# Storing every second low weight part of the first token group for reuse, and new gather rates by stage, in a three-group gMLP, SSD and PEER block

## The chip, the cores and the metric

The kernel runs on one core of one Trainium2 chip. The metric is the device time of one execution in microseconds (us); smaller is better. TensorE (PE in the rows, PEld for its weight loads), VectorE (DVE), ScalarE (ACT), GpSimd (POOL) and SyncE (SP, which only issues transfers here) each run their own list of instructions in a fixed order and wait for each other by semaphores.

## The reference

One block over 1024 tokens with 1024 features, all in fp32:

```
h = x @ w_in                                   # uv, z, xbc, dt, gates
ya = gmlp_branch(uv, ...) @ gm_w_out           # gelu, layer norm, 128-token mixing
yb = ssd_branch(z, xbc, dt, ...) @ ssd_w_out   # conv, chunked scan, gated norm
x1 = layer_norm(ALPHA * x + (g0 * ya + g1 * yb) @ w_o)
q = x1 @ w_q                                   # 8 heads, two keys each
experts, gates = two-level top-16 of 128 x 128 keys, softmax
ch = sum over 128 chosen experts of gates * gelu(u_tab[e] . x1) * v_tab[e]
ple = sigmoid(x1 @ ple_w_gate + b) * (p @ ple_w_proj)
out = layer_norm(ALPHA * x1 + ch + ple)
```

## The kernel before

**Groups.** The tokens go through in three groups of 256, 384 and 384 (`GROUPS`). `front(gi)` does everything up to the choice of experts for one group. For the first two groups the experts are then gathered row by row from DRAM (`experts_u`, `experts_v`); for the third they are computed densely over all 16384 experts (`dense_scores`, `dense_gates`, `dense`). In the rows below, front 0 runs from 0 to 520 us, front 1 from 520 to 1345, front 2 from 1345 to 2600, the dense part up to 3673, and what is left to the end. Within a front I call the parts after what they compute: the gMLP part (`phase` 0), the SSD part (`phase` 1), the merge of both branches (also `phase` 1 before), the query part with `w_o`, `w_q` and `ple` (`phase` 2). Fronts 1 and 2 have these from 520, 712, 1066, 1140 and from 1345, 1548, 1922, 2005 us on. The gate tables of the third group (`phase` 3) start at about 2310, the dense part is `phase` 4.

**Weights.** Products are split for fp32 precision: every operand is a high part in float32r and a low part that holds the rest, and `mm3` multiplies three times (lines 155 to 157). `weights` loads one tile of 512 KB (`raw`, on SP's queue), ACT rounds it to `whi` (line 149), DVE subtracts to get `wlo` (line 150). There are 676 such tiles; the 140 tiles of a front come again in each of the three fronts, 12 of the 420 are half size. The tiles of the dense part (`peer_uT`, `peer_vd`) come once.

**Gathers.** One gather brings 128 rows of 4 KB (512 KB) by an indirect DMA that POOL issues (line 837) into one of 12 `row` tiles (`ring`). A gather of `peer_u` is used by one DVE product (line 856). Four gathers of `peer_v` are used by eight matmuls into `pacc` (line 898; the trace counts each of them as two, so a set of four gathers is a row `x16`). There are 640 of each, 256 of each for the first group and 384 for the second.

**The order.** `front` and `dense` are generators that yield the estimated cost of what they have just written. The loop at the end of `block_kernel` multiplies it by `SIDE[phase]` and writes as many gathers, at 1.47 us each, beside it:

```
for cost in front(gi):
    owed += cost * SIDE[phase[0]]
    ...
    while side and owed > 0:
        step = next(side[0], None)
```

What is still left when `dense` is done is written after it, and ends with `finish` of the last block (lines 800 to 809). A scheduler turns this into the engines' lists, by priority; `tc.high_priority(offset=n)` moves an instruction n places ahead. POOL's list holds gathers and a few plain loads, and a waiting one holds up those behind it.

Of the kernel before, what the change touches and what calls it, by code (L numbers as in the profile page):

```python
# [8 lines left out]
F32 = mybir.dt.float32  # L9
F32R = mybir.dt.float32r  # L10
# [10 lines left out]
KD = D // 128  # L21
# [19 lines left out]
CST = 300  # L41
AHEAD_W = (20, 20)
AHEAD_G = 40
LEAD = 50
UNIT = 5.35
SIDE = (0.82, 0.78, 0.80, 0.66, 0.78)
ALPHA = 2 ** 0.25
# [29 lines left out]
def rows(ap, off, n, parts=128, stride=0):  # L77
    return bass.AP(tensor=ap.tensor, offset=ap.offset + off, ap=[[stride, parts], [1, n]])
# [3 lines left out]
def block_kernel(ctx, tc, a, out):  # L82
# [54 lines left out]
    def split(hi, lo, src):  # L137
        A.copy(hi, src)  # L138
        V.tensor_sub(lo, src, hi.bitcast(F32))  # L139

    def weights(src, k, n):

        raw = wp.tile([128, k, n], F32, name="raw", tag="raw", bufs=4)
        hi = wp.tile([128, k, n], F32R, name="whi", tag="whi", bufs=3)
        lo = wp.tile([128, k, n], F32R, name="wlo", tag="wlo", bufs=3)
        with tc.high_priority(offset=AHEAD_W[0]):
            DMA.dma_start(raw, src)
        with tc.high_priority(offset=AHEAD_W[1]):
            A.copy(hi, raw)  # L149
            V.tensor_sub(lo, raw, hi.bitcast(F32))  # L150
        return hi, lo
# [36 lines left out]
    def normalize(x, st, pool):  # L188
# [13 lines left out]
    def prepare(gi):  # L202

        T = GROUPS[gi][0] * 128
        t0 = 128 * sum(g[0] for g in GROUPS[:gi])
        where = ("left", "right")[gi % 2]
        es = ExitStack()
        xp = es.enter_context(tc.tile_pool(name="xp", bufs=1, side=where))
        xh = xp.tile([128, KD, T], F32R, name="xh")
        xl = xp.tile([128, KD, T], F32R, name="xl")  # L210
        with tc.tile_pool(name="xr", bufs=4, side=where) as xr:
            for k in range(KD):
                raw = xr.tile([128, T], F32, name="xraw")
                DMA.dma_start(raw, a["xT"][:, k, t0:t0 + T])
                split(xh[:, k], xl[:, k], raw)
        tokens[gi] = es, xp, xh, xl

    def front(gi):
# [24 lines left out]
        with tc.tile_pool(name="ga", bufs=1, side=side_) as ga, \  # L243
# [14 lines left out]
            def steps():  # L258
                raw = wp.tile([128, KD, NCOL], F32, name="raw", tag="raw", bufs=4)
                DMA.dma_start(raw, a["w_dt"])  # L260
                dh = wp.tile([128, KD, NCOL], F32R, name="whi", tag="whi", bufs=3)
                dl = wp.tile([128, KD, NCOL], F32R, name="wlo", tag="wlo", bufs=3)
                split(dh, dl, raw)
# [9 lines left out]
                V.tensor_add(dt, pd, dtb[:, None, :].to_broadcast(sh))  # L273
                e, r, q = [ga.tile(sh, F32, name=n) for n in ("e", "r", "q")]
                A.activation(e, dt, AF.Abs)
# [102 lines left out]
        with tc.tile_pool(name="sa", bufs=1, side=side_) as sa, tc.tile_pool(name="sb", bufs=2, side=side_) as sb:  # L378
# [117 lines left out]
            def first_half():  # L496
                for j in range(8):
                    p = channel_major(a["ssd_w_out"][j, 0], yfh, yfl)
                    o = sb.tile([128, T], F32, name="yo")
# [60 lines left out]
        for c in range(NB):  # L560
            DMA.dma_start(x1[:, c], a["x"][t0 + c * 128:t0 + c * 128 + 128, :])
        plb = q0.tile([128, 1024], F32, name="plb")
        qa_es = ExitStack()
        lq = qa_es.enter_context(tc.tile_pool(name="lq", bufs=1, side=side_))
        lg = lq.tile([128, 1024], F32, name="lg")
        lb = lq.tile([128, 1024], F32, name="lb")
# [3 lines left out]
        DMA.dma_start(lb, rows(a["ln1_b"], 0, 1024))  # L570
        DMA.dma_start(plb, rows(a["ple_b_gate"], 0, 1024))
        ph = lq.tile([128, 2, T], F32R, name="ph")
# [12 lines left out]
        with tc.tile_pool(name="qa", bufs=1, side=side_) as qa, tc.tile_pool(name="qb", bufs=2, side=side_) as qb:  # L585
# [98 lines left out]
    def select(gi, c):  # L684
# [303 lines left out]
    def dense(gi, t0, NB, xh, xl):  # L988
        T = NB * 128
        with tc.tile_pool(name="ea", bufs=1) as ea, tc.tile_pool(name="eb", bufs=2) as eb, \  # L990
# [13 lines left out]
            def piece(i2):  # L1004
# [153 lines left out]
```

## Time and profile before

| | |
|---|---|
| median of 3 runs | 3757.99 us (3755.95 to 3758.19) |
| the profiled execution | 3754.28 us, its span 3752.6 us |
| PE busy | 3439.9 us, 92% of the span |
| DVE busy | 2935.7 us, 78% |
| moved by DMA | 1183.88 MB, 315 GB/s in the mean |

A row of the windows gives, for a stretch in us from the span's start, its length, the busy time of each engine with its instructions, the granted TensorE clock as a share of full speed, the mean busy share of the 16 DMA engines, and GB/s. A row of the timeline gives start, duration, engine, line, operation, tiles, and in brackets the engine's idle time before it and what ended it.

### The profile page before, as it was taken

To read this page: it belongs to the slowest core of one execution; us is meant where nothing else is said; L and a number is where in the kernel's file an instruction comes from. 1 tells how busy PE (TensorE), PEld (TensorE's weight loads), DVE (VectorE), ACT (ScalarE), POOL (GpSimd) and SP (SyncE) were. 2 spreads that over 40 slices of the span, in tenths; PEclk is the share of its full clock that TensorE was granted. 3 is DMA by queue.
4 is the path that set the end of the run, shared out by engine and by line. 5 is a ranking of instruction groups with operands and counts; after the bars stand their busy time and mean duration, and the time that the engine had idled before them with its cause. 6 is when DMAs were issued, how large, how long until landed. Compare 5 with 4: busy or idle time off the path is not lost. (4 is left out here: it accounts for less than half of the span.)

```text
span 3752.6 us, 59429 instructions
## 1 busy us (share of the span) xinstructions
PE 3439.9 (92%) x21390; PEld 2939.4 (78%) x21390; DVE 2935.7 (78%) x6823; ACT 1754.2 (47%) x2671; POOL 1569.2 (42%) x1310
## 2 busy tenths in 40 slices
PE   9899996999998988999987989889989999999995
PEld 8888896888887977888777878777768878778771
DVE  6677898898987989894698999997676676676652
ACT  6888443475752333475742334675333323233220
POOL 0000004744455444543455455334455455455544
PEclk9999998999999999999999999999999999999997
DMA  6444647989899787989899899899999999999987
GB/s 212 160 164 160 229 174 249 389 308 356 311 369 391 288 305 285 358 308 323 295 326 337 302 337 371 329 335 370 349 378 379 363 360 370 357 365 395 367 313 283
DMA packets 405703, 1183.88 MB, mean 315 GB/s; under 512 B 40736, under 2 KB 135968, under 8 KB 402336
## 3 DMA queue, kind: packets, MB, share of 16 engines
q0 software_dynamic: 187488, 682.71, 48.5%
q1 hardware_dynamic: 217200, 494.76, 36.8%
q8 instruction: 168, 2.75, 0.3%
q10 hardware_dynamic: 720, 2.62, 0.2%
q14 instruction: 127, 1.04, 0.1%
HBM read 1121.01 MB, written 58.92 MB: 314 GB/s over the span
## 5 line engine op out<-in xcount | busy, mean ns | idle before, releaser
L149 ACT CAST whi<-raw 128x1024 fp32r<-128x1024 f32 (+1 forms) x676 | 700.5, 1041 | 1127.2 <-PE mm L156 582.2
L837 POOL DMA_INDIRECT row<-in_peer_u_dram,idx x640 | 796.3, 1244 | 1004.3 <-PE pacc L898 376.2
L157 PE MATMUL mm<-xh,wlo 128*128 128x384 f32 (+2 forms) x3160 | 1055.3, 335 | 57.4 <-DVE wlo L150 50.5
L150 DVE TENSOR_TENSOR wlo<-raw,whi 128x1024 fp32r<-128x1024 f32 (+1 forms) x676 | 817.1, 1211 | 371.0 <-ACT whi L149 298.7
L155 PE MATMUL mm<-xh,whi 128*128 128x384 f32 (+2 forms) x3160 | 1060.6, 336 | 38.0 <-ACT whi L149 27.2
L156 PE MATMUL mm<-xl,whi 128*128 128x384 f32 (+2 forms) x3160 | 1046.8, 331 | 0.6 <-DVE xl L139 0.6
L837 POOL DMA_INDIRECT row<-in_peer_v_dram,idxT x640 | 758.9, 1186 | 681.9 <-DVE row L856 210.9
L856 DVE SCALAR_TENSOR_TENSOR row<-row,x1b 128x1024 f32<-128x1024 f32 x640 | 773.6, 1217 | 22.9 <-DMA row<-in_peer_u_dram,idx 18.5
L155 PEld LDWEIGHTS mm<-xh,whi 128*128 128x128 f32 (+1 forms) x3160 | 606.9, 192 | 93.4 <-ACT whi L149 51.5
L157 PEld LDWEIGHTS mm<-xh,wlo 128*128 128x128 f32 (+1 forms) x3160 | 606.1, 192 | 78.1 <-DVE wlo L150 60.1
L156 PEld LDWEIGHTS mm<-xl,whi 128*128 128x128 f32 (+1 forms) x3160 | 606.3, 192 | 9.5 <-issue 2.8
L898 PE MATMUL pacc<-row,zw 128*32 128x512 f32 x2560 | 321.3, 621 | 39.2 <-DMA row<-in_peer_v_dram,idxT 39.1
L155 PE MATMUL po<-whi,ewh 128*128 128x512 f32 x768 | 313.9, 409 | 20.1 <-DVE eacc L1051 17.9
L156 PE MATMUL po<-wlo,ewh 128*128 128x512 f32 x768 | 309.4, 403 | 17.1 <-DVE wlo L150 17.0
L157 PE MATMUL po<-whi,ewl 128*128 128x512 f32 x768 | 308.2, 401 | 0.0
L898 PEld LDWEIGHTS pacc<-row,zw 128*32 128x32 f32 x2560 | 68.5, 111 | 193.9 <-issue 140.6
L155 PEld LDWEIGHTS po<-whi,ewh 128*128 128x128 f32 x768 | 147.3, 192 | 86.3 <-DVE eacc L1051 19.9
L156 PEld LDWEIGHTS po<-wlo,ewh 128*128 128x128 f32 x768 | 147.5, 192 | 50.4 <-DVE wlo L150 18.5
L852 POOL DMA_DIRECT2D x1b<-x x5 | 3.0, 606 | 434.2 <-DMA x<-x 434.1
L138 ACT CAST ewh<-ew 128x384 fp32r<-128x384 f32 x128 | 65.6, 513 | 242.4 <-DVE ew L1019 175.3
L157 PEld LDWEIGHTS po<-whi,ewl 128*128 128x128 f32 x768 | 147.4, 192 | 36.1
L981 PE MATMUL mt<-o,o 128*128 128x128 f32 x768 | 148.9, 302 | 15.1 <-DVE o L979 6.0
(275 smaller groups left out, 5609.3 us busy)
## 6 DMA issues: line engine op xcount, KB each, us to landing
raw<-in_peer_uT_dram SPq DMA_DIRECT2D x128, 512.0 KB
raw<-in_peer_vd_dram SPq DMA_DIRECT2D x128, 512.0 KB
raw<-in_w_xbc_dram SPq DMA_DIRECT2D x96, 512.0 KB
raw<-in_w_g_dram SPq DMA_DIRECT2D x48, 512.0 KB
raw<-in_w_z_dram SPq DMA_DIRECT2D x48, 512.0 KB
raw<-in_ssd_w_out_dram SPq DMA_DIRECT2D x48, 512.0 KB
raw<-in_w_q_dram SPq DMA_DIRECT2D x48, 512.0 KB
g<-gt SPq DMA_DIRECT2D x24, 1024.0 KB
```

The costliest lines, as they stand in the source:

```text
L138: A.copy(hi, src)
L149: A.copy(hi, raw)
L150: V.tensor_sub(lo, raw, hi.bitcast(F32))
L155: PE.matmul(p, lhsT=lh, rhs=rh, start=start, stop=False, skip_group_check=skip)
L156: PE.matmul(p, lhsT=lh, rhs=rl, start=False, stop=False, skip_group_check=skip)
L157: PE.matmul(p, lhsT=ll, rhs=rh, start=False, stop=stop, skip_group_check=skip)
L837: g = POOL.indirect_dma_start(out=t, out_offset=None, in_=a[tab], in_offset=bass.IndirectOffsetOnAxis(ap=ix, axis=0))
L852: POOL.dma_start(x1, x1_d[gi, c])
L856: u = V.scalar_tensor_tensor(t, t, 1.0, x1, op0=OP.mult, op1=OP.mult, accum_out=act[:, k:k + 1])
L898: return PE.matmul(pacc[q * 32:q * 32 + 32, h * 512:h * 512 + 512], lhsT=zws[z][:, q, r % 4, :], rhs=ts[q][:, h * 512:h * 512 + 512], star ...
L981: PE.matmul(p[:, i, :], lhsT=o1, rhs=o2, start=True, stop=True)
```

## The change

In front 0 every second weight tile (`turn[0] % 2 == 0`) also stores its `wlo` to a DRAM tile of its own, by a DMA on POOL's queue. In fronts 1 and 2 a tile that is found in `kept` loads this `wlo` back, again on POOL's queue and 80 places ahead (`AHEAD_L`), instead of subtracting on DVE. `raw` and `whi` are as before. The one set of three `wlo` buffers becomes two sets of two: `wlo0` and `wlo1`. In front 0 and for the dense part's tiles the sets alternate; in fronts 1 and 2 loaded tiles use `wlo1` and subtracted ones `wlo0`. The gather rates `SIDE` change for four of the five stages, and the merge gets one of its own (`phase` 5). To make room, other tiles become fewer or are shared: `xraw` 4 to 3, `ewh` and `ewl` 13 to 11, `e`, `r`, `q`, `yo`, `plb` and `ixf` move into tiles that exist already.

```diff
-AHEAD_W = (20, 20)
+AHEAD_W, AHEAD_L = (20, 20), 80
-SIDE = (0.82, 0.78, 0.80, 0.66, 0.78)
+SIDE = (0.70, 0.82, 0.68, 0.66, 0.86, 1.1)
...
+        key = (src.tensor.name, src.offset)
+        keep = front_of[0] == 0 and turn[0] % 2 == 0
+        again = key in kept
         raw = wp.tile([128, k, n], F32, name="raw", tag="raw", bufs=4)
         hi = wp.tile([128, k, n], F32R, name="whi", tag="whi", bufs=3)
-        lo = wp.tile([128, k, n], F32R, name="wlo", tag="wlo", bufs=3)
+        turn[0] += 1
+        own = front_of[0] == 0 or "peer_" in src.tensor.name
+        at = turn[0] % 2 if own else int(again)
+        lo = wp.tile([128, k, n], F32R, name="wlo", tag=f"wlo{at}", bufs=2)
         with tc.high_priority(offset=AHEAD_W[0]):
             DMA.dma_start(raw, src)
+        with tc.high_priority(offset=AHEAD_L):
+            if again:
+                POOL.dma_start(lo, kept[key])
         with tc.high_priority(offset=AHEAD_W[1]):
             A.copy(hi, raw)
-            V.tensor_sub(lo, raw, hi.bitcast(F32))
+            if not again:
+                V.tensor_sub(lo, raw, hi.bitcast(F32))
+        if keep:
+            kept[key] = dram.tile([128, k, n], F32R, name=f"lo{turn[0]}")
+            POOL.dma_start(kept[key], lo)
...
+        phase[0] = 5
         mp_es = ExitStack()
...
-                ready[i2] = [eb.tile([128, T], F32R, name=n, bufs=I2B + 5) for n in ("ewh", "ewl")]
+                ready[i2] = [eb.tile([128, T], F32R, name=n, bufs=I2B + 3) for n in ("ewh", "ewl")]
```

POOL's list at the start of the gathers, in front 1, before (`x1b` is the block's input row, `idx` and `idxT` the expert numbers):

```order
L852 DMA x1b<-x_0_0_5316 128x1024
L852 DMA x1b<-x_0_1_5318 128x1024
L837 DMA row<-in_peer_u_dram,idx_0_7225 128x1024 x70
L837 DMA row<-in_peer_v_dram,idxT_0_7226 128x1024
L837 DMA row<-in_peer_u_dram,idx_0_7225 128x1024
```

and with the change (`lo_...` are the DRAM tiles):

```order
L160 DMA wlo<-lo_214 128x1024
L160 DMA wlo<-lo_280 128x1024
L160 DMA wlo<-lo_379 128x1024
L160 DMA wlo<-lo_467 128x1024
L160 DMA wlo<-lo_570 128x1024
L160 DMA wlo<-lo_652 128x1024
L861 DMA row<-in_peer_u_dram,idx_0_7360 128x1024 x5
L160 DMA wlo<-lo_736 128x1024
L861 DMA row<-in_peer_u_dram,idx_0_7360 128x1024 x5
L160 DMA wlo<-lo_820 128x1024
L861 DMA row<-in_peer_u_dram,idx_0_7360 128x1024 x5
L160 DMA wlo<-lo_912 128x1024
```

A load now stands after about every five gathers, 140 in all, and 70 stores stand ahead of the first gather.

DVE's list in the merge of front 1, before (`row` products are the gathers' users, `ya` and `ml` the merge itself):

```order
L150 TENSOR_TENSOR wlo<-raw,whi 128x1024
L139 TENSOR_TENSOR ml<-ya,mh 128x384
L150 TENSOR_TENSOR wlo<-raw,whi 128x1024
L856 SCALAR_TENSOR_TENSOR row,act<-row,x1b 128x1024
L545 TENSOR_TENSOR sg<-sg,rrow 128x384
L856 SCALAR_TENSOR_TENSOR row,act<-row,x1b 128x1024
L150 TENSOR_TENSOR wlo<-raw,whi 128x1024
L547 TENSOR_TENSOR ya<-ya,mm 128x384
L150 TENSOR_TENSOR wlo<-raw,whi 128x1024
```

and with the change:

```order
L164 TENSOR_TENSOR wlo<-raw,whi 128x1024
L880 SCALAR_TENSOR_TENSOR row,act<-row,x1b 128x1024
L569 TENSOR_TENSOR ya<-ya,mm 128x384
L911 COPY zw_139<-wT 64x4x4 x2
L570 TENSOR_TENSOR ya<-ya,sg 128x384
L571 TENSOR_TENSOR ya<-ya,m0t 128x384
L880 SCALAR_TENSOR_TENSOR row,act<-row,x1b 128x1024
L139 TENSOR_TENSOR ml<-ya,mh 128x384
L164 TENSOR_TENSOR wlo<-raw,whi 128x1024
```

Half of the subtractions are gone from between the others; over the whole program DVE has 676 of them before and 536 after.

The end of PE's list before (`po` are the last products of the dense part):

```order
L155 MATMUL po<-whi,ewh 128x512
L156 MATMUL po<-wlo,ewh 128x512
L157 MATMUL po<-whi,ewl 128x512
L898 MATMUL pacc<-row,zw_139 32x512 x32
L898 MATMUL pacc<-row,zw_138 32x512 x32
L898 MATMUL pacc<-row,zw_139 32x512 x32
```

and with the change:

```order
L172 MATMUL po<-whi,ewh 128x512
L173 MATMUL po<-wlo,ewh 128x512
L174 MATMUL po<-whi,ewl 128x512
L172 MATMUL po<-whi,ewh 128x512
L173 MATMUL po<-wlo,ewh 128x512
L174 MATMUL po<-whi,ewl 128x512
L922 MATMUL pacc<-row,zw_139 32x512 x16
```

Of 96 `pacc` matmuls (48 gathers) behind the last `po`, 16 (8 gathers) are left. By the same list the dense part holds those of 272 gathers of `peer_v` instead of 228, and all before it 360 instead of 364. The group of eight ahead of the last sixteen stands 18 `po` matmuls before the end.

## Rows read from the trace of the kernel before

**Rows 1.** The page: span, busy time, share and instructions of two engines.

```profile
span 3752.6 us, 59429 instructions
PE 3439.9 (92%) x21390; PEld 2939.4 (78%) x21390; DVE 2935.7 (78%) x6823; ACT 1754.2 (47%) x2671; POOL 1569.2 (42%) x1310
```

**Rows 2.** Windows, by stage.

```profile
0.00:520.00 520.00, 477.82 (x3807) 458.36 (x3808) 384.87 (x929) 367.05 (x597) 2.21 (x9) 0.97 0.55 186
520.00:712.00 192.00, 161.14 (x966) 153.53 (x965) 182.06 (x476) 72.04 (x95) 89.90 (x64) 0.92 0.74 272
712.00:1066.00 354.00, 341.85 (x2254) 300.99 (x2253) 313.47 (x620) 243.05 (x390) 172.87 (x143) 0.99 0.89 330
1066.00:1140.00 74.00, 70.46 (x417) 64.42 (x418) 61.47 (x101) 26.31 (x34) 42.60 (x35) 0.98 1.00 382
1140.00:1345.00 205.00, 187.27 (x1314) 162.75 (x1314) 176.23 (x571) 65.17 (x99) 97.02 (x79) 0.96 0.89 333
1345.00:1548.00 203.00, 178.71 (x1082) 153.70 (x1082) 190.02 (x580) 77.53 (x103) 100.94 (x79) 0.94 0.84 308
...
2005.00:2310.00 305.00, 272.59 (x1751) 243.25 (x1750) 285.64 (x965) 106.37 (x144) 147.29 (x119) 0.96 0.89 328
...
2600.00:3673.00 1073.00, 1026.32 (x5243) 811.89 (x5245) 702.88 (x1084) 325.69 (x435) 541.09 (x457) 0.97 0.97 363
3673.00:3752.60 79.60, 34.76 (x193) 6.47 (x192) 15.25 (x29) 5.63 (x7) 38.83 (x40) 0.68 0.77 291
```

**Rows 3.** Waits of PE from 520 to 2310 us: total, times, longest.

```profile
PE mm L157 <- DVE wlo L150: 51.3, 24, 14.2
...
PE mm L156 <- DVE wlo L150: 17.0, 8, 5.4
```

**Rows 4.** Windows around the longest of these waits, and of high traffic.

```profile
622.00:640.00 18.00, 5.20 (x17) 5.20 (x18) 18.00 (x43) 1.32 (x3) 5.00 (x4) 0.53 0.49 155
...
680.00:712.00 32.00, 32.00 (x183) 32.00 (x182) 32.00 (x50) 8.83 (x11) 27.43 (x16) 1.00 1.03 412
```

**Rows 5.** Timeline of PE at the end.

```profile
3672.38 0.40 PE L156 MATMUL po<-wlo,ewh 128*128 128x512 f32 x1
3672.62 0.39 PE L157 MATMUL po<-whi,ewl 128*128 128x512 f32 x1
3672.94 3.64 PE L898 MATMUL pacc<-row,zw 128*32 128x512 f32 x32
...
3738.09 2.96 PE L898 MATMUL pacc<-row,zw 128*32 128x512 f32 x16 [2.44 <-DMA row<-in_peer_v_dram,idxT]
```

**Rows 6.** Timeline of DVE at the end: the first instruction of the last finish.

```profile
3741.10 1.22 DVE L802 TENSOR_TENSOR x1b<-x1b,pacc 128x1024 f32<-128x1024 f32 x1 [43.87 <-PE pacc L898]
```

**Rows 7.** Timeline of PE within the dense part: one set of four gathers.

```profile
3651.98 1.92 PE L898 MATMUL pacc<-row,zw 128*32 128x512 f32 x16
```

**Rows 8.** The chain that ended last: longest and shortest of its five gathers.

```profile
3688.32 9.59 DMA row<-in_peer_v_dram,idxT
...
3731.78 6.26 DMA row<-in_peer_v_dram,idxT
```

**Rows 9.** The page's groups: the subtraction.

```profile
L150 DVE TENSOR_TENSOR wlo<-raw,whi 128x1024 fp32r<-128x1024 f32 (+1 forms) x676 | 817.1, 1211 | 371.0 <-ACT whi L149 298.7
```

**Rows 10.** Timeline of PE in front 1: the pace of a front's products.

```profile
616.17 0.34 PE L155 MATMUL mm<-xh,whi 128*128 128x384 f32 x1
616.35 0.34 PE L156 MATMUL mm<-xl,whi 128*128 128x384 f32 x1
```

**Rows 11.** Timeline of POOL: a plain load of 512 KB, and a gather.

```profile
3707.14 0.59 POOL L796 DMA_DIRECT2D row<-in_ln_g_dram  x1
...
3709.89 0.97 POOL L837 DMA_INDIRECT row<-in_peer_v_dram,idxT  x1 [0.30 <-issue]
```

**Rows 12.** Waits of POOL from 520 to 2310 us.

```profile
POOL row L837 <- DVE row L856: 274.9, 120, 12.0
POOL row L837 <- PE pacc L898: 274.6, 60, 10.8
```

More of the change, by code (lines that the diff above doesn't have):

```diff
@@ L139, in split @@
         V.tensor_sub(lo, src, hi.bitcast(F32))
+    kept, turn = {}, [0]
     def weights(src, k, n):
+        key = (src.tensor.name, src.offset)
+        keep = front_of[0] == 0 and turn[0] % 2 == 0
+        again = key in kept
         raw = wp.tile([128, k, n], F32, name="raw", tag="raw", bufs=4)
         hi = wp.tile([128, k, n], F32R, name="whi", tag="whi", bufs=3)
-        lo = wp.tile([128, k, n], F32R, name="wlo", tag="wlo", bufs=3)
+        turn[0] += 1
+        own = front_of[0] == 0 or "peer_" in src.tensor.name
+        at = turn[0] % 2 if own else int(again)
+        lo = wp.tile([128, k, n], F32R, name="wlo", tag=f"wlo{at}", bufs=2)
         with tc.high_priority(offset=AHEAD_W[0]):
             DMA.dma_start(raw, src)
+        with tc.high_priority(offset=AHEAD_L):
+            if again:
+                POOL.dma_start(lo, kept[key])
         with tc.high_priority(offset=AHEAD_W[1]):
             A.copy(hi, raw)
-            V.tensor_sub(lo, raw, hi.bitcast(F32))
+            if not again:
[3 more added lines that the diff above has]
+            POOL.dma_start(kept[key], lo)
         return hi, lo
@@ L195, in normalize @@
         A.activation(x, x, AF.Identity, scale=rs, bias=nm)
+    front_of = [None]
     ps, ps_es, phase, tk_, selects = {}, [None], [0], [None], []
@@ L210, in prepare @@
         xl = xp.tile([128, KD, T], F32R, name="xl")
-        with tc.tile_pool(name="xr", bufs=4, side=where) as xr:
+        with tc.tile_pool(name="xr", bufs=3, side=where) as xr:
             for k in range(KD):
@@ L231, in front @@
         phase[0] = 0
+        front_of[0] = gi
         tk_es = ExitStack()
@@ L261, in steps @@
                 dh = wp.tile([128, KD, NCOL], F32R, name="whi", tag="whi", bufs=3)
-                dl = wp.tile([128, KD, NCOL], F32R, name="wlo", tag="wlo", bufs=3)
+                dl = wp.tile([128, KD, NCOL], F32R, name="wlo", tag="wlo0", bufs=2)
                 split(dh, dl, raw)
@@ L273, in steps @@
                 V.tensor_add(dt, pd, dtb[:, None, :].to_broadcast(sh))
-                e, r, q = [ga.tile(sh, F32, name=n) for n in ("e", "r", "q")]
+                erq = gb.tile([128, T], F32, name="erq", tag="t1", bufs=3)
+                e, r, q = [erq[:, n * NB * NCOL:(n + 1) * NB * NCOL].rearrange("p (c h) -> p c h", c=NB)
+                           for n in range(3)]
                 A.activation(e, dt, AF.Abs)
@@ L498, in first_half @@
                     p = channel_major(a["ssd_w_out"][j, 0], yfh, yfl)
-                    o = sb.tile([128, T], F32, name="yo")
+                    o = sb.tile([128, T + 3], F32, name="xin")[:, :T]
                     A.copy(o, p)
@@ L561, in front @@
             DMA.dma_start(x1[:, c], a["x"][t0 + c * 128:t0 + c * 128 + 128, :])
-        plb = q0.tile([128, 1024], F32, name="plb")
+        lg = q0.tile([128, 1024], F32, name="lg")
         qa_es = ExitStack()
         lq = qa_es.enter_context(tc.tile_pool(name="lq", bufs=1, side=side_))
-        lg = lq.tile([128, 1024], F32, name="lg")
         lb = lq.tile([128, 1024], F32, name="lb")
@@ L570, in front @@
         DMA.dma_start(lb, rows(a["ln1_b"], 0, 1024))
-        DMA.dma_start(plb, rows(a["ple_b_gate"], 0, 1024))
         ph = lq.tile([128, 2, T], F32R, name="ph")
@@ L612, in front @@
             for u in range(16):
+                if u == 4:
+                    plb = lg
+                    DMA.dma_start(plb, rows(a["ple_b_gate"], 0, 1024))
                 p = channel_major(a["w_q"][u], xh, xl)
@@ L762, in select @@
             ixT = idxT_t[gi, c].rearrange("p (n q r) -> p n q r", n=PARTS, q=4)
-            ixf = [tk.tile([128, PARTS, PP], F32, name=f"ixf{p}") for p in range(PARTS)]
+            ixf = [wide.rearrange("p h k n -> p (h k n)")[:, p * 128:p * 128 + 128].rearrange(
+                "p (n k) -> p n k", n=PARTS) for p in range(PARTS)]
             for p in range(PARTS):
```

## The prediction

> **What bounds the kernel now.** The page first: PE is busy in 3439.9 of 3752.6 us, DVE in 2935.7 [rows 1]. A share over the whole span hides stages with different limits, so the windows come next. In the SSD part of front 1 PE is busy in 341.9 of 354 us and nothing can be won there but the products themselves. In the gMLP parts (520 to 712 and 1345 to 1548) and the query part of front 2, DVE is busy in 182 of 192, 190 of 203 and 286 of 305 us, PE in less, and the granted clock is 0.92, 0.94 and 0.96 [rows 2]. There PE waits for DVE: from 520 to 2310 us it waits 51.3 + 17.0 = 68.3 us, in 32 waits, for a `wlo` [rows 3]. The longest, 14.2 us, shows what follows one: in the 18 us around it DVE is busy all the time, and the granted clock is 0.53, that is mostly at 1.2 instead of 2.4 GHz [rows 4]. From 2600 us on PE is again the busiest, beside transfers at 363 GB/s [rows 2]. The last 79.6 us are another case: the dense part's products are done at 3673, and PE does 48 gathers' products as they land, busy in 34.8 us at a clock of 0.68 [rows 2, 5]. So the end is a tail of gathers with nothing beside it, and then the last finish, from 3741.1 to 3752.6, 11.5 us [rows 6].
>
> **The change, part by part.** The sum is made against the profiled execution, 3754.3 us.
>
> *The tail.* With the new rates 8 gathers of `peer_v` are left behind the last `po` instead of 48. The last gathers can't be issued at will: of the 12 `row` tiles four hold layer-norm rows by then, so the last four gathers wait for the set that stands 18 `po` matmuls ahead of the end, 18 x 0.24 = 4.3 us [rows 5]. From there four issues of 0.97 + 0.30 us [rows 11] and a landing of 6.3 to 9.6 us [rows 8], taken as 8, make 13; less the 4.3, 9 us behind the last `po`, then 1.9 us of products [rows 7] and the finish of 11.5 us. That is 22 us instead of 79.6: **-58**. (18 if the gathers land as fast as the fastest, 30 if the finish has to wait for the dense part's own layer norm.)
>
> *What the tail did is done elsewhere.* The dense part gets 44 gathers more, the fronts 4 fewer. A set of four costs PE 1.92 us at full clock [rows 7]: 11 sets are 21 us, one set less is 2: **+19**. The tail's products were no cheaper, but at the end there was nothing beside them.
>
> *The subtractions.* 140 fewer at 1.21 us [rows 9] take 140 x 1.21 = 169 us (a little less, since 8 are half as long) from DVE, spread over fronts 1 and 2, where it is the busier engine in three stages. On the path they are worth at most what PE waits for them: 68.3 us [rows 3]. Every second tile no longer asks DVE at all, and for the others DVE has half the backlog; but its other work (gather products, top-16) stays, and with the same waits for ACT's `whi`. Ends 0 and 68; I take half, **-34**. The rates of the gMLP and query parts, lower now, work the same way and are in this half.
>
> *The clock.* In the four stages where it is 0.92 to 0.96 it costs 15 + 8 + 12 + 12 = 48 us (192 x 0.08, 205 x 0.04, 203 x 0.06, 305 x 0.04) [rows 2]. About half of PE's idle time there is these waits, so some 24 us hang on them; with half of the waits gone **-12** (0 to -24).
>
> *The loads.* No operation like them stands in the trace at this place; the nearest is a plain load on the same queue, 0.59 us of POOL with 0.3 of issue [rows 11], and 6.3 to 9.6 us from issue to landing for a gather of the same size [rows 8]. POOL is busy in 97 to 173 us of stages of 205 and 354 us [rows 2], so 140 x 0.9 = 126 us have room. What counts is whether a load lands in time. `wlo1` has two buffers, so a load waits until the loaded tile four places earlier is used up, and three tiles of 24 products lie ahead of its use: 72 x 0.176 = 12.7 us at the pace of [rows 10]. Less 0.9 and 8 that leaves 4 us. In token-major stretches some have only about two tiles ahead, 9 us, and are late by around 1 us; a late one costs its clock too. Nothing if all are in time; with some 15 late by under 1 us, **+12**. Behind a load that waits for its buffer the gathers wait as well. That is covered: POOL already waits 275 us for DVE's products and 275 us for `pacc` in these fronts, up to 12.0 us at a time [rows 12], so gathers run well ahead of use; without that cover each load would hold up a row's product by its wait.
>
> *Traffic.* 136 x 0.524 + 4 x 0.262 = 72 MB are loaded in fronts 1 and 2 and half of that is stored in front 0. Front 0 runs at 186 GB/s [rows 2]; 36 MB over 520 us add 70, beside an idle POOL. In the SSD part of front 1 some 33 loads (17 MB in 354 us) add 49 to 330 GB/s; in its merge, with the rate of 1.1, 382 GB/s would go beyond the 412 GB/s that a stretch with PE busy throughout shows [rows 2, 4], and what doesn't fit moves into the query part, where there are 333 and fewer gathers now. Slower landings and a store that holds a `wlo` in front 0: 0 to +40, taken **+7**. The smaller sets (`xraw`, `ewh`, `ewl`) and shared tiles (`yo`, `plb`, `ixf`, `erq`) I cost at nothing: ACT is busy in 326 of 1073 us of the dense part [rows 2] and hides a later cast. If it doesn't, each of the 16 steps loses up to the 4.3 us of 18 `po`, 70 us in all.
>
> Here a rule of the Trainium skill speaks against the change. The rows show 412 GB/s over 32 us with PE never idle, and 363 over the dense part [rows 2, 4]. "DMA: Bandwidth & Descriptors", section "Where 436 GB/s comes from", says that for transfers between HBM and SBUF the HBM share of a core, about 358 GB/s, binds. This case's trace doesn't agree for a core that streams alone; by that rule the end would be an estimated 3770 us (the fourth rival's sum with 358), so slower, and by the rows the queues still have room.
>
> Sum: -58 + 19 - 34 - 12 + 12 + 7 = -66, so 3688 against 3754.3. The median of the runs, 3758.0, is 3.7 above the profiled execution; I forecast **3692** for it.
>
> **The rivals.** A change of under 0.2% (7.5 us) is what a measurement of this kernel can't tell from none.
>
> 1. *The loads give back what the subtractions gave.* DVE is relieved, but PE waits for loads as long as it did for `wlo`, mostly in the gMLP parts, where gathers wait for a DVE that is 95% busy and loads stand behind them. Then only the tail is left: -58 + 19 + 3 = -36, **3722**. For it: the small margin of 4 us. Against it: three tiles of lead, and less work on DVE.
>
> 2. *The loads are late: slower than before.* One mechanism: POOL works its list in order, a gather in front of a load waits up to 12.0 us for a DVE product [rows 12], and this eats the margin. 30 loads late by 4 us, with half-clock stretches behind them, take 30 x 4 = 120 instead of 12: 3692 + 108 = **3800**. It decides from some 20 such loads on (66 + 12 = 78 us). Against it: most of POOL's waits are those of gathers that are ahead.
>
> 3. *More is won.* All 68 us and 24 of clock, and loads in time: -58 + 19 - 92 + 3 = -128, **3630**.
>
> 4. *The queues become the bound.* All bytes after 520 us are 1183.9 - 97 (186 GB/s x 520 us) = 1087 MB, and 72 more are 1159. At the dense part's 363 GB/s these take 3193 us: 520 + 3193 + 12 = **3725**. Against it: the 412 GB/s.
>
> 5. *The gain and a few late loads cancel:* half of the second rival's price, **3750 to 3765**.
>
> **How the numbers follow.** The forecast (3655 to 3715) 0.57; rival 1, 0.13; rival 4, 0.08; rival 3, 0.07; rival 5, 0.04; rival 2, 0.11. Faster by over 0.2%: 0.57 + 0.13 + 0.08 + 0.07 = 0.85; the same 0.04; slower 0.11. The range of 3640 to 3762 leaves out the second and most of the third rival, 0.17; the forecast's own is the 3655 to 3715.
>
> **What would show it.** In the trace of the changed kernel: from the last `po` to the end 18 to 30 us, no long row of `pacc` waits there; dense part some 20 us longer or less, by what its waits do; `wlo` of DVE as a cause of PE's waits from 520 to 2310 at some 34 us instead of 68; a new cause, DMA `wlo<-lo`, at some 10 us; granted clock of the gMLP parts 0.95 or more; DMA at 370 to 390 GB/s in fronts 1 and 2. The prediction is wrong if DMA `wlo<-lo` is PE's first cause of waits, if `pacc` waits for rows before the end, or if the dense part shows waits for `ewh`.

## The result and the profile after

The changed kernel takes 3733.41 us (median of 4 runs, 3723.69 to 3734.77), the kernel before beside it 3758.09 (4 runs, 3755.95 to 3761.96): a ratio of 0.9928, 95% interval 0.9913 to 0.9944. Faster, by 25 us where 66 were forecast. The profiled execution took 3733.71 us, its span is 3732.0.

The page of the changed kernel, lines that answer to [rows 1], and the line of its DMA packets:

```profile
span 3732.0 us, 59553 instructions
...
PE 3432.0 (92%) x21390; PEld 2941.5 (79%) x21390; DVE 2790.4 (75%) x6683; ACT 1752.4 (47%) x2672; POOL 1646.2 (44%) x1520
...
DMA packets 435944, 1292.43 MB, mean 346 GB/s; under 512 B 44096, under 2 KB 139328, under 8 KB 432576
```

DVE's 140 subtractions are gone (6823 to 6683 instructions) and it is busy 145 us less, and 108.5 MB are moved more: 36 stored and 72 loaded, as counted.

Windows of the changed kernel by stage: front 0 in four parts, front 1 from 551 to 1384, front 2 to 2344, both as one row, then dense part and tail.

```profile
0.00:125.00 125.00, 110.91 (x878) 108.31 (x879) 71.25 (x154) 67.95 (x95) 10.79 (x25) 0.97 0.80 267
125.00:371.00 246.00, 218.89 (x1711) 205.51 (x1709) 177.55 (x384) 215.44 (x376) 14.88 (x28) 0.94 0.64 208
...
423.00:551.00 128.00, 117.34 (x909) 112.78 (x909) 106.91 (x392) 59.40 (x96) 10.69 (x20) 0.96 0.82 280
551.00:723.00 172.00, 153.64 (x897) 146.27 (x897) 150.17 (x394) 69.54 (x92) 85.97 (x77) 0.95 0.88 329
723.00:1075.00 352.00, 336.08 (x2222) 294.81 (x2222) 287.48 (x597) 243.62 (x391) 190.91 (x172) 0.99 0.99 374
1075.00:1168.00 93.00, 78.78 (x469) 66.97 (x467) 56.93 (x102) 27.03 (x35) 52.43 (x51) 0.96 1.04 404
1168.00:1384.00 216.00, 197.82 (x1368) 176.05 (x1368) 165.31 (x592) 70.99 (x106) 97.51 (x95) 0.95 0.99 370
1384.00:1552.00 168.00, 158.06 (x966) 138.07 (x967) 158.28 (x510) 69.58 (x94) 93.08 (x82) 0.97 0.95 357
...
551.00:2344.00 1793.00, 1642.07 (x10561) 1452.82 (x10561) 1435.69 (x3790) 867.09 (x1302) 922.47 (x840) 0.97 0.97 362
...
2628.00:3711.00 1083.00, 1032.09 (x5310) 799.37 (x5312) 697.07 (x1076) 318.39 (x427) 564.77 (x495) 0.97 0.99 371
3711.00:3732.00 21.00, 4.23 (x33) 0.77 (x32) 14.28 (x25) 5.63 (x7) 0.52 (x1) 0.66 0.44 166
```

The same stretches of the kernel before, in rows that [rows 2] cut otherwise: front 0, fronts 1 and 2, the dense part.

```profile
0.00:531.00 531.00, 488.82 (x3901) 469.36 (x3902) 395.77 (x997) 370.55 (x602) 2.21 (x9) 0.97 0.55 187
...
531.00:2335.00 1804.00, 1652.34 (x10596) 1454.84 (x10594) 1576.60 (x3924) 867.02 (x1300) 882.33 (x710) 0.96 0.88 322
...
2628.00:3673.00 1045.00, 1002.72 (x5121) 791.35 (x5124) 690.77 (x1064) 318.53 (x426) 528.94 (x447) 0.98 0.97 362
```

In fronts 1 and 2 DVE is busy 141 us less, and the stretch is only 11 us shorter. PE stands idle there for 1804 - 1652 = 152 us before and 1793 - 1642 = 151 after; what is won are 10 us of PE's busy time, at a clock of 0.97 instead of 0.96. The column to read is the one ahead of GB/s: the queues' share went from 0.88 to 0.97.

Waits in the changed kernel: first PE, DVE and POOL from 551 to 2344, then, behind the last gap, PE in the dense part.

```profile
PE mm L174 <- DMA wlo<-lo: 15.5, 9, 3.9
PE mm L172 <- ACT whi L162: 14.8, 14, 3.3
PE mm L173 <- DMA wlo<-lo: 14.1, 3, 6.9
PE mt L805 <- DVE sel L753: 13.9, 4, 6.2
PE mt L467 <- DVE cbm L451: 13.3, 7, 3.9
PE mm L174 <- DVE wlo L164: 10.1, 10, 3.1
PE pacc L922 <- DMA row<-in_peer_v_dram,idxT: 10.1, 5, 3.8
...
PE mm L173 <- DVE wlo L164: 7.1, 3, 2.8
...
DVE row L880 <- DMA row<-in_peer_u_dram,idx: 40.1, 22, 3.7
...
POOL wlo L160 <- PE mm L174: 188.9, 65, 12.1
POOL row L861 <- PE pacc L922: 164.8, 60, 13.9
POOL row L861 <- DVE row L880: 157.8, 84, 7.2
...
PE po L172 <- DVE eacc L1075: 31.0, 7, 15.4
PE po L173 <- DVE wlo L164: 16.7, 5, 5.3
```

PE's 68.3 us of waits for a subtracted `wlo` [rows 3] are down to 17.2. What came instead: 29.6 us for a loaded `wlo`, and more waits for other work of DVE (`sel` 13.9 us, 2.7 before; `cbm` 13.3, 1.1 before). DVE itself waits 40.1 us for gathered rows; in the kernel before, from 530 to 2334, it was this:

```profile
DVE row L856 <- DMA row<-in_peer_u_dram,idx: 3.3, 3, 2.3
```

The end, on PE's timeline:

```profile
3710.61 0.40 PE L174 MATMUL po<-whi,ewl 128*128 128x512 f32 x1
3710.94 1.93 PE L922 MATMUL pacc<-row,zw 128*32 128x512 f32 x16
3716.36 2.37 PE L922 MATMUL pacc<-row,zw 128*32 128x512 f32 x16 [3.49 <-DMA row<-in_peer_v_dram,idxT]
```

The tail of [rows 5] is gone: 21 us from the last `po` to the end, with one wait of 3.49 us.

Stage lengths in us, of three pairs of profiled executions. Front 1 begins with DVE's first `st` of it, the gates (the gate tables ahead of the dense part) with ACT's first `gt`, the dense part with ACT's first `ew`, and the tail at the end of the last `po`.

| | front 0 | fronts 1, 2 | gates | dense | tail |
|---|---|---|---|---|---|
| before | 530.6 | 1804.1 | 293.2 | 1045.1 | 79.6 |
| after | 551.0 | 1792.6 | 284.7 | 1082.7 | 21.0 |
| `before_again` | 532.1 | 1805.8 | 292.6 | 1047.6 | 79.5 |
| `change_again` | 553.8 | 1798.7 | 285.1 | 1079.1 | 20.8 |
| `before_third` | 531.3 | 1814.0 | 296.9 | 1040.6 | 80.5 |
| `change_third` | 551.6 | 1795.5 | 287.0 | 1079.0 | 21.9 |

So in the first pair +20.4 - 11.5 - 8.5 + 37.6 - 58.6 = -20.6, the difference of the spans.

### The profile page after: what moved, and what is told of

Same layout as the page of the kernel before. It is cut to its first block, busy times and chain, and to the rows that moved or that the text cites. A ratio compares the mean times of both kernels' runs of the same rounds, so it can differ in the third digit from the quotient of the medians.

```text
span 3732.0 us, 59553 instructions
## 1 busy us (share of the span) xinstructions
PE 3432.0 (92%) x21390; PEld 2941.5 (79%) x21390; DVE 2790.4 (75%) x6683; ACT 1752.4 (47%) x2672; POOL 1646.2 (44%) x1520
## 4 chain that ended last, share of the span: by engine, by line
PE 35%; DVE 14%; DMA 9%; ACT 3%; issue 3%; another core or an unknown queue 1%; POOL 0%; SPq 0%; POOLq 0%; DVEq 0%; ACTq 0%
PE mm L172 6%; PE mm L174 6%; PE mm L173 6%; PE pacc L922 4%; PE po L172 4%; DVE row L880 4%; PE po L174 4%; PE po L173 4%; DMA ew<-s 3%; DVE wlo L164 2%; PE mt L1005 2%; ACT whi L162 1%; DMA vit<-vi 1%; DMA row<-in_peer_u_dram,idx 1%; DMA wlo<-lo 1%
## 5 line engine op out<-in xcount | busy, mean ns | idle before, releaser
L861 POOL DMA_INDIRECT row<-in_peer_u_dram,idx x640 | 776.3, 1213 | 684.8 <-PE pacc L922 255.8
L861 POOL DMA_INDIRECT row<-in_peer_v_dram,idxT x640 | 737.6, 1153 | 634.7 <-DVE row L880 217.2
L164 DVE TENSOR_TENSOR wlo<-raw,whi 128x1024 fp32r<-128x1024 f32 x536 | 649.6, 1212 | 341.1 <-ACT whi L162 311.9
L174 PEld LDWEIGHTS mm<-xh,wlo 128*128 128x128 f32 (+1 forms) x3160 | 606.3, 192 | 55.0 <-DVE wlo L164 20.3
L922 PE MATMUL pacc<-row,zw 128*32 128x512 f32 x2560 | 312.6, 606 | 13.6 <-DMA row<-in_peer_v_dram,idxT 13.6
L167 POOL DMA_DIRECT2D lo<-wlo x70 | 37.5, 535 | 480.0 <-DVE wlo L164 406.4
L160 POOL DMA_DIRECT2D wlo<-lo x140 | 81.1, 580 | 232.1 <-PE mm L174 198.0
```

The costliest lines, as they stand in the source:

```text
L160: POOL.dma_start(lo, kept[key])
L167: POOL.dma_start(kept[key], lo)
L174: PE.matmul(p, lhsT=ll, rhs=rh, start=False, stop=stop, skip_group_check=skip)
L861: g = POOL.indirect_dma_start(out=t, out_offset=None, in_=a[tab], in_offset=bass.IndirectOffsetOnAxis(ap=ix, axis=0))
L922: return PE.matmul(pacc[q * 32:q * 32 + 32, h * 512:h * 512 + 512], lhsT=zws[z][:, q, r % 4, :], rhs=ts[q][:, h * 512:h * 512 + 512], star ...
```

## The experiments

Each time stands beside the kernel before in the same batch, run on the same chip, since batches differ: it took 3720 us in the first and fourth, which I call the quicker ones, and 3758 to 3769 in the others. Ratios are compared across batches with care, stage lengths of fronts and gates only between like batches. A stage length is that of the one profiled execution, and executions of a kernel differ by up to 20 us; where it matters, the medians stand beside it.

### Parts of the change alone (before: 3719.82)

`rates_only`, the kernel before with

```diff
-SIDE = (0.82, 0.78, 0.80, 0.66, 0.78)
+SIDE = (0.70, 0.82, 0.68, 0.66, 0.86, 1.1)
...
+        phase[0] = 5
```

> The kernel before with the new gather rates and nothing else of the change. Theory A (the dense part's extra 17 us and the merge's 10 us come from the new rates, front 0's 20 us from the stores): tail 80 to about 20 us, dense part +36 us, merge of front 1 +8 us, front 0 unchanged; together about -15 us, 3743. Theory B (the extra comes from the smaller and shared buffers, in front 0 and in the dense part): dense part +20 us only, merge unchanged, together about -40 us, 3718.

`stores_loads_only`, the changed kernel with

```diff
-SIDE = (0.70, 0.82, 0.68, 0.66, 0.86, 1.1)
+SIDE = (0.82, 0.78, 0.80, 0.66, 0.78, 0.78)
```

> The changed kernel with the gather rates of before (0.78 in the merge too): stores, loads and the smaller buffers alone. Theory A: front 0 +20 us, fronts 1 and 2 together -30 us, dense part and tail as before; about 3748. Theory B: front 0 +20 us, dense part +15 us; about 3763.

`loads_no_stores`, the changed kernel without stores; the loads read the weights themselves as low parts:

```diff
-            kept[key] = dram.tile([128, k, n], F32R, name=f"lo{turn[0]}")
-            POOL.dma_start(kept[key], lo)
+            kept[key] = src
```

> The changed kernel without the stores in front 0; the loads of fronts 1 and 2 read the weight tensor itself, the same bytes at the same places in the order (so the low parts that are loaded hold the whole weights, and the results differ from the reference's). Theory A: front 0 falls from 540 us back to about 522, the rest as in the changed kernel; 3715. Theory B: front 0 stays at 540; 3733.

`buffers_only`, the changed kernel with the rates as before, one set of three `wlo`, and nothing kept:

```diff
-        keep = front_of[0] == 0 and turn[0] % 2 == 0
+        keep = False
...
-        lo = wp.tile([128, k, n], F32R, name="wlo", tag=f"wlo{at}", bufs=2)
+        lo = wp.tile([128, k, n], F32R, name="wlo", tag="wlo", bufs=3)
```

> The changed kernel with no stores, no loads, one set of three wlo buffers and the old rates: what is left are the smaller and shared buffers (xraw 3, ewh and ewl 11, yo, erq, plb and ixf in other tiles). Theory A: front 0 +3 us, dense part unchanged; about 3762. Theory B: front 0 +15 us, dense part +15 us; about 3788.

| | us | ratio, interval | front 0 | fronts 1, 2 | gates | dense | tail |
|---|---|---|---|---|---|---|---|
| `rates_only` | 3701.26 | 0.9951, 0.9930 to 0.9972 | 530.5 | 1785.2 | 278.5 | 1089.1 | 22.2 |
| `stores_loads_only` | 3728.31 | 1.0019, 1.0005 to 1.0033 | 548.2 | 1768.0 | 274.8 | 1050.6 | 78.7 |
| `loads_no_stores` | 3701.05 | 0.9946, 0.9927 to 0.9966 | 538.8 | 1782.9 | 275.5 | 1081.5 | 21.1 |
| `buffers_only` | 3725.48 | 1.0016, 1.0005 to 1.0028 | 533.8 | 1793.7 | 283.1 | 1047.5 | 79.7 |

The rates alone bring the tail's gain and the dense part's price: 1089.1 us with them and without the smaller buffers, 1047.5 the other way round, as Theory A had it. Stores and loads alone are no gain: fronts 1 and 2 and the gates win 1793.7 + 283.1 - 1768.0 - 274.8 = 34 us over the smaller buffers, and front 0 and the dense part give 18 of it back. The spans of the two differ by 17.5 us in its favour, the medians by 3 against it (the profiled execution of `buffers_only`, 3739.52, is its longest), so the 34 may be some 20 too large. With the new rates beside them the loads win little more in fronts 1 and 2 than the rates do without them (1782.9 and 1785.2). So in this batch the rates alone (0.9951) gain as much as the change without its stores (0.9946), and the stores would come on top: storing and loading low parts shows no gain of its own here. The rates alone weren't run in a slower batch, and the change itself in no quicker one. Front 0's price is some 3 us of buffers, 9 to 12 of the stores, and 5 of what else `loads_no_stores` has over `buffers_only` (the split `wlo` sets, the first late loads, the rates), which weren't tried apart.

### The change again, with fewer kept parts or with other rates (before: 3768.53)

`before_again` and `change_again` are the two kernels once more.

> The kernel before, once more, so that its stages can be set beside those of the experiments on the same chip. Both theories: the time of the runs of before on this chip; front 0 530 us, fronts 1 and 2 some 2077, dense part some 1047, tail 80.

> The changed kernel, once more. Both theories: the ratio measured already, 0.993; front 0 some 548, fronts 1 and 2 some 2058 and so no better than with the stores left out, dense part some 1083, tail 21.

`front_rates_of_before`:

```diff
-SIDE = (0.70, 0.82, 0.68, 0.66, 0.86, 1.1)
+SIDE = (0.82, 0.78, 0.80, 0.66, 0.86, 0.78)
```

> The changed kernel with the rates of before in all fronts (0.82, 0.78, 0.80, 0.66, and 0.78 in the merge) and 0.86 only in the dense part; no gather stands behind the last po in the order. Theory A (gathers and loads collide in the merges, where the rate of 1.1 asks for more than the queues carry): merges 84 and 93 us instead of 95 and 115, fronts 1 and 2 together 2043 instead of 2058, dense part 1085 to 1095, tail 15 to 20; ratio 0.988. Theory B (the merges only take over work that would stand in other stages, so their length says nothing): fronts 1 and 2 together 2058 as with the new rates, ratio 0.993.

`keep_outside_ssd`:

```diff
-        keep = front_of[0] == 0 and turn[0] % 2 == 0
+        keep = front_of[0] == 0 and turn[0] % 2 == 0 and phase[0] in (0, 2)
```

> The changed kernel in which only tiles of the gMLP and the query part are stored and loaded, none of the SSD part and the merge, where PE and not DVE is the busier engine. Theory A (stores and loads cost by their traffic and help only where DVE is behind): front 0 gets 8 us back, the SSD parts stay, merges get 5 us back each, and the gMLP parts keep their gain; ratio 0.988. Theory B (the help of the loads is the smaller backlog of DVE everywhere): fronts 1 and 2 lose 15 us or more, ratio 0.995 or above.

`before_again` took 3759.4 us, `change_again` 3740.06, ratio 0.9934 (0.9914 to 0.9954): the result holds. `front_rates_of_before` took 3726.04, 0.9892 (0.9869 to 0.9915), `keep_outside_ssd` 3728.74, 0.9896 (0.9873 to 0.9920). The first takes 11.5 us off fronts 1 and 2 (1787.2). Most of what it does is a shift: its merges, without the rate of 1.1, take 83.9 and 93.1 us instead of 91.6 and 114.5, and the gMLP part of front 2 takes 192.4 instead of 169.4. Its gates win nothing (295.2), and front 0 is 7 us shorter in this execution, for which no edit accounts. The second leaves out the kept parts of SSD parts and merges, and takes 8 us off fronts 1 and 2 (1790.7) and 6 off front 0.

### Which queue, and how full (before: 3763.75)

`loads_on_sp`:

```diff
-                POOL.dma_start(lo, kept[key])
+                DMA.dma_start(lo.bitcast(F32), kept[key].bitcast(F32))
```

> The changed kernel with one line changed: the 140 late loads are issued by SP, behind the plain loads of raw, instead of by POOL, among the gathers. Theory C: on POOL's list a load that waits for its wlo1 buffer (188.9 us of such waits in the fronts of the changed kernel) holds up the gathers behind it, and the rows come late to DVE, which waits 40.1 us for them there. Then DVE's waits for a row in the fronts fall to 15 us or less, fronts 1 and 2 get 10 to 20 us shorter, and the ratio to the kernel before is 0.988 to 0.990. Rival D: rows and loads are late because landings got slower with the bytes on the queues, wherever they are issued. Then DVE waits some 40 us for rows still, fronts 1 and 2 keep their length within 6 us, and the ratio is 0.993. A load that waits on SP's list holds up the loads of raw instead; if that is worse, PE's waits for whi grow and the ratio goes above 0.996.

`fewer_dense_loads` (`same` holds a piece of `xh` while a tile of `peer_vd` is set up; by the trace 100 tiles, 52.4 MB, fall away, not the 64 of the text):

```diff
+        once = bool(same) and turn[0] % 2 == 0
-        raw = wp.tile([128, k, n], F32, name="raw", tag="raw", bufs=4)
+        raw = same[0] if once else wp.tile([128, k, n], F32, name="raw", tag="raw", bufs=4)
...
-            DMA.dma_start(raw, src)
+            if not once:
+                DMA.dma_start(raw, src)
```

> The changed kernel, but every second weight tile of the dense part (64 of 128, 33.5 MB) isn't loaded: ACT and DVE split a piece of xh in its place, so the output is another. Instructions of PE, ACT, DVE and POOL stay as they are. Theory: the dense part is longer by 33 to 38 us instead of 19 because the 44 gathers put there come on top of queues that are full (share 0.99). Then without these bytes the dense part falls from 1080 us to 1065 or less. Rival: the surplus is PE's own, its products and the clock after short waits. Then the dense part stays within 5 us of 1080.

`front_rates_and_keep` has the edits of `front_rates_of_before` and `keep_outside_ssd`, `rates_keep_and_sp` that of `loads_on_sp` besides.

> The changed kernel with the gather rates of the fronts as before and low parts kept only outside the SSD parts, both at once. Each alone gave 0.989 to 0.990. Theory: they heal different stretches (the gMLP and query parts, and the SSD parts with front 0's stores), so together 0.985 to 0.987. Rival: both take the same thing away, bytes and gathers from full queues, and together they give no more than 0.988 to 0.990.

> The kernel front_rates_and_keep with the late loads on SP instead of POOL. Theory C: another 5 to 10 us, 0.983 to 0.985. Rival D: the same as front_rates_and_keep within 0.002.

`loads_on_sp` took 3747.7 us, 0.9964 (0.9952 to 0.9975). Its waits from 547 to 2333, DVE, POOL and SP's queue:

```profile
DVE row L880 <- DMA row<-in_peer_u_dram,idx: 53.3, 42, 3.6
...
POOL row L861 <- PE pacc L922: 363.7, 64, 17.4
...
SPq L160 <- PE mm L174: 237.6, 90, 9.3
```

POOL's 188.9 us of waits at loads are gone, and it waits so much longer for `pacc`, that is for PE: its gathers were ahead anyhow. DVE's waits for rows don't fall (40.1 to 53.3). Theory C fell: no cost shows of what stands behind a load on POOL's list. On SP's list the loads hold up those of `raw`: PE's waits for `whi` there are 20.4 against 14.8 us in their largest row.

`fewer_dense_loads` took 3718.92 us, 0.9892 (0.9868 to 0.9915). The window of its dense part, and PE's waits there:

```profile
2634.00:3688.00 1054.00, 1020.48 (x5312) 792.53 (x5314) 696.74 (x1077) 319.33 (x427) 573.21 (x494) 0.99 0.93 331
```

```profile
PE po L174 <- DVE eacc L1079: 25.3, 5, 11.1
PE po L175 <- DVE wlo L166: 6.8, 3, 2.6
```

With PE, DVE and POOL at the same instructions the dense part takes 1053 us instead of 1079 to 1083: PE's idle time falls from 51 to 34 us, its busy time from 1032 to 1020 at a clock of 0.99 instead of 0.97. It was the loads that it waited for, as the theory said. In the changed kernel ACT has this wait there, and in this run none for a `raw`:

```profile
ACT whi L162 <- DMA raw<-in_peer_vd_dram: 40.7, 4, 17.1
```

Whether these loads were late because the queues were full isn't shown apart from this, since 100 of the 128 tiles of `peer_vd` are what fell away. (By the medians and ratios the whole kernel gains 0.0036 to 0.0054, that is 14 to 20 us; its profiled execution, 3710.23, is its fastest.)

`front_rates_and_keep` took 3725.72 us, 0.9901 (0.9881 to 0.9921), no better than either edit alone: its rival was right. `rates_keep_and_sp` took 3742.13, 0.9947 (0.9927 to 0.9966), a loss from SP's list once more.

### Bytes or buffers (before: 3720.66)

`fewer_front_loads` (by the page 70.8 MB fall away, not the 49 of the text):

```diff
+        once = again and bool(prev) and tuple(prev[-1].shape) == (128, k * n)
-        raw = wp.tile([128, k, n], F32, name="raw", tag="raw", bufs=4)
+        flat = prev[-1] if once else wp.tile([128, k * n], F32, name="raw", tag="raw", bufs=4)
+        prev[:] = [flat]
+        raw = flat.rearrange("p (k n) -> p k n", k=k)
...
-            DMA.dma_start(raw, src)
+            if not once:
+                DMA.dma_start(raw, src)
```

> The changed kernel, but where a low part is loaded, the plain load of raw is left out for the tiles of full size: ACT rounds the raw tile before it once more. SP has 94 plain loads (49 MB) fewer in fronts 1 and 2; the output is another. The low parts are loaded as before, on POOL. Rival D (bytes): the relief of fronts 1 and 2 was lost to slower landings, since the loads came on top of queues that were nearly full. Then the time from the start of front 1 to the gates falls from 1793 us to 1780 or less, DVE's waits for a row (44.6 us) fall by half, and PE's for a loaded wlo (29.6 us) to 15 or less. Theory E (buffers and order): the loads are late since a wlo1 buffer comes free late, and DVE's other work is next in line; bytes don't matter. Then 1787 to 1797 us, and PE's waits for a loaded wlo stay at 25 to 33.

`idle_tile_stores`:

```diff
-            POOL.dma_start(kept[key], lo)
+            if not idle:
+                idle.append(ring.tile([128, 1024], F32, name="row", tag="row"))
+                POOL.memset(idle[0], 0.0)
+            POOL.dma_start(kept[key], idle[0][:, :k * n].rearrange("p (k n) -> p k n", k=k))
```

> The changed kernel, but the 140 stores of front 0 write an idle tile of zeros instead of the wlo tile, so that no store waits for a wlo and none holds its buffer; bytes, queue and places stay (the low parts loaded later are zeros, so the output is another). Theory 1: front 0 is 14 to 21 us longer than before since stores hold wlo buffers. Then front 0 falls from 551 us to 540 or less, as with no stores at all (538.8). Theory 2: it is the bytes and issues themselves. Then front 0 stays at 546 to 554 us.

`keep_in_gmlp_only`, with the rates of `front_rates_of_before` and

```diff
-        keep = front_of[0] == 0 and turn[0] % 2 == 0
+        keep = front_of[0] == 0 and turn[0] % 2 == 0 and phase[0] == 0
```

> The changed kernel with the gather rates of the fronts as before and low parts kept only in the gMLP parts (the start of front 0), where PE waited longest for wlo. If bytes are what costs, the fewest loads at the place of the longest waits give most: 0.985 to 0.988. If the relief of the query parts counts as much, it falls behind the two kernels at 0.989: 0.990 to 0.993.

`fewer_front_loads` took 3674.11 us, 0.9866 (0.9844 to 0.9887), `idle_tile_stores` 3736.13, 1.0037 (1.0022 to 1.0052). In fronts 1 and 2 these two differ by the plain loads alone (and so by how long a `raw` buffer is held), and they ran on one chip. Fronts 1 and 2 as one window, then the waits there, first of `fewer_front_loads`:

```profile
549.00:2299.00 1750.00, 1632.71 (x10564) 1451.46 (x10563) 1433.29 (x3782) 865.25 (x1300) 933.19 (x840) 0.97 0.92 332
```

```profile
DVE row L884 <- DMA row<-in_peer_u_dram,idx: 15.6, 12, 2.4
...
PE mm L176 <- ACT whi L166: 17.0, 12, 3.3
PE mm L177 <- DMA wlo<-lo: 14.5, 5, 5.3
```

and of `idle_tile_stores`, whose windows begin with three of front 0:

```profile
0.00:151.00 151.00, 118.66 (x909) 114.58 (x909) 71.00 (x154) 68.22 (x95) 39.18 (x78) 0.93 1.01 403
151.00:395.00 244.00, 218.54 (x1678) 205.38 (x1678) 177.93 (x384) 215.19 (x376) 0.00 (x0) 0.92 0.47 148
...
445.00:568.00 123.00, 115.65 (x920) 111.39 (x920) 106.81 (x392) 59.42 (x95) 2.70 (x5) 0.99 0.67 229
...
568.00:2353.00 1785.00, 1644.93 (x10563) 1459.26 (x10562) 1434.27 (x3787) 867.42 (x1301) 927.12 (x840) 0.96 0.96 364
```

```profile
DVE row L883 <- DMA row<-in_peer_u_dram,idx: 49.5, 23, 4.4
...
PE mm L177 <- DMA wlo<-lo: 15.5, 9, 4.5
PE mm L176 <- DMA wlo<-lo: 14.3, 2, 7.7
PE mm L175 <- ACT whi L162: 13.8, 14, 3.3
```

1785 against 1750 us, DVE's waits for rows 49.5 against 15.6, PE's for loaded low parts 29.8 against 14.5, with the same loads on the same list and the same buffers. PE's waits for `whi` don't differ in the same way (13.8 and 17.0), nor do DVE's (69.0 and 69.5), so it isn't that ACT got its `raw` sooner. By the medians the kernels are 62 us apart, 19.5 of them in front 0, so 35 isn't too much. Rival D holds, Theory E falls: about 71 MB cost 35 us in these fronts. The traces of the quicker batches also give the median time from a gather's issue to its landing (last number), in these windows first of `idle_tile_stores`, then of `fewer_front_loads`:

```profile
row<-in_peer_u_dram,idx POOLq DMA_INDIRECT x382, 9.6
row<-in_peer_v_dram,idxT POOLq DMA_INDIRECT x312, 9.0
```

```profile
row<-in_peer_u_dram,idx POOLq DMA_INDIRECT x382, 7.8
row<-in_peer_v_dram,idxT POOLq DMA_INDIRECT x312, 7.1
```

The first batch agrees: 7.5 and 7.5 in `buffers_only` and 7.8 and 8.0 in `rates_only`, without late loads, 8.8 and 8.5 in `stores_loads_only` and 9.5 and 8.6 in `loads_no_stores`, with them. So landings did get slower with the bytes.

For front 0 both numbers of `idle_tile_stores` missed. Without a `wlo` to wait for, the stores crowd into the first 151 us, at a share of 1.01 and 403 GB/s, and this start is 35 us longer than before (116.4); the rest of front 0, without stores, has its old length (416.9 us against 414.2). So stored bytes alone can cost that much. How much of the 9 to 12 us in the changed kernel is bytes and how much a `wlo` held by its store stays open.

`keep_in_gmlp_only` took 3691.43 us, 0.9920 (0.9899 to 0.9941), in the range for a relief that counts in the query parts as much.

### Once more on one chip (before: 3760.44)

> The kernel before once more, for its stage lengths on this chip. Either 3720 us, with gates of 275 us, or 3760 with gates of 293.

> The changed kernel once more. Theory: the tail's gain is the same on every chip, and the fronts' gain isn't, since on the quicker chips PE waits less for DVE: at 3720 us the ratio is 0.996 to 0.999, at 3760 us 0.993 again. Rival: the ratio is the same on every chip, 0.992 to 0.995.

> keep_in_gmlp_only once more, beside the change. If added bytes are what the relief was lost to, it beats the change on the same chip by 0.003 or more; if not, they are within 0.002.

`before_third` took 3765.03 us, `change_third` 3738.44, 0.9946 (0.9929 to 0.9963), `keep_in_gmlp_third` 3736.26, 0.9931 (0.9910 to 0.9952). The batch was a slower one again, so the change's own ratio in a quicker one stays unknown. Keeping in the gMLP parts alone isn't ahead of the change by the 0.003 expected: it saves 12 us in front 0 (539.3 against 551.6), 5 in dense part and tail, and loses 21 in fronts 1 and 2 and gates, where the waits of PE for a subtracted `wlo` are back (33.5 + 25.1 us in its two rows). Fewer bytes help only as far as they don't cost the relief.

## Why the prediction was right in direction and wrong in size

- **The tail, -58.** Right: -58.6. That the 21.0 us are so near the 22 is in part luck: they are 7.7 to the end of the last products, where 10.9 were worked out, and 13.2 of finish, where 11.5 were.
- **Relief and clock, -34 and -12.** The mechanism is there: PE's waits for a subtracted `wlo` fell from 68.3 to 17.2 us, further than to the 34 forecast, and the granted clock of the gMLP parts rose from 0.92 and 0.94 to 0.95 and 0.97. Yet fronts 1 and 2 won only 11.5, 7.1 and 18.5 us in the three pairs, 12 in the mean, where this and the loads came to 34.
- **The loads, +12.** Too small. Twelve late loads cost 29.6 us, up to 6.9 each, where some 15 under 1 us were expected. With 71 MB fewer beside them they cost 14.5 us (`fewer_front_loads`), near the 12. That gathers behind a waiting load are covered was right (`loads_on_sp`).
- **What the tail did, +19.** Too small: +37.6, +31.5 and +38.4. In the first pair PE is busy 29.4 us longer there, at a clock of 0.97 instead of 0.98, and idle 8.6 us longer. Its products were counted, the 23 MB of the 44 gathers weren't, in a stage whose queues were at a share of 0.97 before [rows 2].
- **Traffic, +7 of 0 to +40.** This step failed, and the misses of the fronts and the loads, and part of that of the dense part, come from it. It read 412 GB/s in a stretch of 32 us, itself at a share of 1.03 [rows 4], as what the queues can do and saw room at 330 to 363 GB/s. The share stood in the next column: 0.89 in the SSD part, 1.00 in the merge, 0.97 in the dense part [rows 2]. With the loads the fronts went from 0.88 to 0.97, gathers took 8.5 to 9.6 us to land instead of 7.5 to 8.0 (in the quicker batches), and rows and low parts came late. The size by `fewer_front_loads` is 35 us for 71 MB; added to the 12 won in fronts 1 and 2 that is 47, about the 46 forecast for relief and clock without any cost of bytes. (It takes the price from a quicker batch to the slower.) By `fewer_dense_loads` 52.4 MB are worth 14 us (by the ratios) to 30 (by the stage) in the dense part, so 44 gathers of 0.524 MB, 23 MB, some 6 to 13: with the 19 that is 25 to 32 of the 31.5 to 38.4 measured, so up to 13 us aren't explained.
- **Front 0,** within the same +7: +20.4, +21.7 and +20.3, of which buffers alone take 3, and stores 9 to 12. The smaller buffers, put at nothing, took some 6 us of the whole kernel (`buffers_only`, 1.0016).
- **The gates** had no term and won 8.5, 7.5 and 9.9 us; `stores_loads_only` won them too, without the rates. Why wasn't tried.

With the first pair's numbers: -58.6 + 37.6 - 11.5 - 8.5 + 20.4 = -20.6 where -66 was forecast. The fourth rival, queues as the bound at 3725, named the queues, at 8 in 100. That its 3725 is near the 3733 is luck: at its 363 GB/s 71 MB would be worth 195 us, and they were worth 35, so the queues make things late and don't bound the kernel. The signs given ahead also spoke: a loaded `wlo` is PE's first cause of waits in the fronts.

Of the versions tried, `front_rates_of_before` (0.9892), `keep_outside_ssd` (0.9896) and both together (0.9901) are in the mean ahead of the change (0.9928, 0.9934, 0.9946); in the same batch the first is at 0.9869 to 0.9915 and the change at 0.9914 to 0.9954, so a small gain over the change is likely.

## What to carry to other kernels

Here trading an engine's work for bytes paid only as far as the queues had time: read their share of busy time by stage, and not the GB/s, before calling a transfer free. At a share of 0.9 and more each MB taken out here was worth about 0.3 to 0.6 us on the path, though no row of waits names full queues: it came out as late rows and late low parts, and as other names in the list of waits. And run each part of a change alone: in the first batch the rates alone gained as much as the rates with the loads. When an engine is relieved, look at the idle time of the engine that waited for it, not at the wait that vanished: here 51 us of one wait went, and PE stood idle as long as before.

## What the runs showed of the hardware

A full share isn't one rate: 1.04 went with 404 GB/s in the merge, 0.99 with 371 in the dense part, 0.97 with 362 in fronts 1 and 2, 1.01 with 403 beside stores in front 0. Batches differ by 1% for one and the same kernel (before at 3720 and at 3758 to 3769 us), and not evenly: front 0 of `rates_only` took 530.5 us in a quicker one and that of the kernel before 530.6 to 532.1 in the slower ones, while fronts 1 and 2 of the kernel of `keep_in_gmlp_only` took 1771.4 us in a quicker and 1810.8 in a slower one, its gates 274.8 and 292.9. What sets them apart wasn't found. It isn't shown to be the chip: the record has chip 4 for the first batch (3720) and for the second (3769) alike. Nor is one number of MB one price: with 36 MB of stores crowded into it the start of front 0 took 35 us more, with 71 MB taken out of fronts 1 and 2 these took 35 us less.
